# Two heads of an attention tile: their TensorE products issued head after head, or by turns

## The chip, the core and the metric

The kernel runs on one core of one Trainium2 chip. A core has five engines, each with an instruction queue of its own, that wait for each other through semaphores: TensorE (PE in the profile, its weight loads in a row of their own, PEld), VectorE (DVE), ScalarE (ACT), GpSimd (POOL) and SyncE (SP, which here only issues DMA transfers). The metric is the device time of one execution in microseconds (us); lower is better.

## The reference, cut to what matters

The reference is one decoder layer over 256 tokens of width 2048, in float32: a SwiGLU feed-forward half-step, a mixer, and a second feed-forward half-step, each followed by a layer normalisation. The mixer projects the tokens into queries, keys, values and the input of a convolution branch. Attention and convolution are computed from these and joined by one output projection.

Attention has 16 query heads of 64 features and 2 key and value heads. Tokens stand in two blocks of 128. A query of block b sees keys of block b-1 and of its own block, no more than 127 tokens back:

```
scores = einsum('bnqhgd,bnkhd->bnhgqk', qb, kb) * ATTN_SCALE
scores = where(valid, scores, finfo(float32).min)
probs  = softmax(concatenate([scores, sink], -1), -1)[..., :-1]
out    = einsum('bnhgqk,bnkhd->bnqhgd', probs, vb)
```

The convolution branch takes a gated product, runs a causal depthwise convolution of 31 taps over it, normalises and applies SiLU.

## The kernel before, in words

**Weights.** Every weight arrives by DMA as float32, in pieces of 128 x 1024. Each piece is split into a rounded part `hi` (ScalarE, line 126) and a remainder `lo` (line 128, on VectorE, or on GpSimd for some pieces of the mixer). TensorE multiplies with both (lines 384 to 386: hi by hi, the two cross products, no lo by lo). The class `Steps` hands the pieces out: `take()` gives the next piece, `release()` gives its buffer back, `step()` ends a step of the program, splits up to two pieces ahead, and calls work that was put off with `st.at(delay, work)`. Each engine is given its instructions in the order in which this Python text issues them; no planner moves them. `st.tensor` and `st.vector` only count, on the host, how much work VectorE has outstanding, to decide at which step convolution taps are issued.

**The mixer.** First a product over tokens gives keys, values and the queries of the first two tiles. Then 14 items follow in the order `ccqqccqqccqqcc`: a "c" is one 128-channel tile of the convolution branch (two products of 48 matmuls, then a sigmoid on ScalarE, line 661, and a gated product on VectorE, line 662), a "q" is the query tile of two heads (one product of 48 matmuls, then a copy with bias on ScalarE, line 762). After every two "c" tiles VectorE gets two chains of 31 taps (line 653). In between, the pieces of attention come due.

**Attention.** There are 8 tiles. Tile `i` holds two heads: head 0 in partitions 0 to 63 of `qT` and `kT`, head 1 in partitions 64 to 127. `attend(i)` puts the scores of a tile into one PSUM tile `sc` of 128 x 2 x 512, head `h` in `sc[:, h]`, a bank of its own. In each bank columns 0 to 127 belong to query block 0 and columns 128 to 383 to query block 1. Three matmuls make a head's scores: the mask, as identity times mask in bf16 over 384 columns (line 677), which also clears the bank, then the product of block 0 (line 678, 128 columns), then that of block 1 (line 679, 256 columns), both in float32 and adding to the mask. A float32 matmul is executed as two loads of weights and two passes, so lines 678 and 679 each show 32 instructions for 16 calls.

From there the steps of `ATT` follow, some 1, 1, 2, 2, 4, 6 and 7 steps after `attend`: the maximum (VectorE, line 691), the exponentials (ScalarE, line 701), the sums and reciprocal (VectorE, lines 708 and 709), the division (ScalarE, line 715), the transposes `turn` (TensorE, line 721) with their copy `pT` (ScalarE, line 724), the product with the values (TensorE, lines 733 to 735) and the copy of the result (lines 740 and 741).

`values()` multiplies the transposed shares by `v`. The weights are the 64 columns of `v` of the head (`v[..][:, r]`), so head 0 writes partitions 0 to 63 of the result and head 1 partitions 64 to 127. Per head there are three float32 matmuls of 128 columns, each again two loads and two passes.

After the 14 items the first half of the output projection starts (`tokens_by`, product lines 384 to 386 on `mh` and `ml`), while VectorE still works on the last two chains of taps.

Of the kernel before, what the change touches and what calls it, by code (L numbers as in the profile page):

```python
# [18 lines left out]
P = 128  # L19
# [8 lines left out]
HD = 64  # L28
# [545 lines left out]
def mixer(tc, nc, env):  # L574
# [6 lines left out]
    with tc.tile_pool(name="mix", bufs=1) as pool:  # L581
# [11 lines left out]
        v = [kvq[:, b, P : 2 * P] for b in range(2)]  # L593
# [3 lines left out]
        def turn_first():  # L597
            tq = psA.tile([P, 2, 512], F32, tag="gu", name="tq")
            for b in range(2):
                for n, col in enumerate((0, 2, 3)):  # L600
                    nc.tensor.transpose(
                        tq[:, n // 2, (n % 2) * S + b * P : (n % 2) * S + (b + 1) * P],
                        kvq[:, b, col * P : (col + 1) * P], ident,
                    )
            nc.scalar.copy(kT, tq[:, 0, :S])
            nc.scalar.copy(qTs[0], tq[:, 0, S:])
            nc.scalar.copy(qTs[1], tq[:, 1, :S])
            attend(0)
            st.at(3, lambda: attend(1))
# [62 lines left out]
        def attend(i):  # L672
            qT = qTs.pop(i)
            sc = psA.tile([P, 2, 512], F32, tag="gu", name="sc")
            for h in range(2):
                r = slice(h * HD, (h + 1) * HD)
                nc.tensor.matmul(sc[:, h, : 3 * P], ident_b, mask, start=True, stop=False)
                nc.tensor.matmul(sc[:, h, :P], qT[r, :P], kT[r, :P], start=False, stop=False)
                nc.tensor.matmul(sc[:, h, P : 3 * P], qT[r, P:], kT[r, :], start=False, stop=True)
            mx = small.tile([P, 2, 2], F32, tag="mx", name="mx")  # L680
            nm = small.tile([P, 2, 2], F32, tag="nm", name="nm")
            se = small.tile([P, 2, 2], F32, tag="se", name="se")
            sm = small.tile([P, 2, 2], F32, tag="sm", name="sm")
            pr = pool.tile([P, 2, 3 * P], F32, tag="pr", name="pr", bufs=2)
            pT = pool.tile([P, 2, 3 * P], F32, tag="pT", name="pT", bufs=2)
            tps = []
            st.tensor(1.6)

            def most():
                for b in range(2):  # L690
                    nc.vector.tensor_reduce(out=mx[:, b], in_=sc[:, :, spans[b]], axis=AX.X, op=ALU.max)
                nc.vector.scalar_tensor_tensor(
                    out=nm, in0=mx, scalar=-SCALE, in1=nsink[:, i], op0=ALU.mult, op1=ALU.min
                )
                nc.vector.tensor_tensor(out=se, in0=psink[:, i], in1=nm, op=ALU.add)
                st.vector(1.5)

            def exps():
                for h in range(2):
                    for b in range(2):  # L700
                        nc.scalar.activation(
                            pr[:, h, spans[b]], sc[:, h, spans[b]], AF.Exp, bias=nm[:, b, h : h + 1], scale=SCALE,
                            accum_out=sm[:, b, h : h + 1],
                        )
                nc.scalar.activation(se, se, AF.Exp)

            def shares():
                nc.vector.tensor_tensor(out=sm, in0=sm, in1=se, op=ALU.add)
                nc.vector.reciprocal(sm, sm)
                st.vector(0.3)  # L710

            def divide():
                for h in range(2):
                    for b in range(2):
                        nc.scalar.mul(pr[:, h, spans[b]], pr[:, h, spans[b]], sm[:, b, h : h + 1])

            def turn():
                tp = psA.tile([P, 2, 512], F32, tag="gu", name="tp")
                for h in range(2):
                    for n in range(3):  # L720
                        nc.tensor.transpose(
                            tp[:, h, n * P : (n + 1) * P], pr[:, h, n * P : (n + 1) * P], ident
                        )
                nc.scalar.copy(pT, tp[:, :, : 3 * P])
                st.tensor(0.7)
                tps.append(tp)

            def values():
                o = tps[0][:, :, 3 * P :]
                st.tensor(0.9)  # L730
                for h in range(2):
                    r = slice(h * HD, (h + 1) * HD)
                    nc.tensor.matmul(o[r, 0], v[0][:, r], pT[:, h, :P], start=True, stop=True)
                    nc.tensor.matmul(o[r, 1], v[0][:, r], pT[:, h, P : 2 * P], start=True, stop=False)
                    nc.tensor.matmul(o[r, 1], v[1][:, r], pT[:, h, 2 * P :], start=False, stop=True)

            def keep():
                o = tps[0][:, :, 3 * P :]
                m = [x_[:, i].rearrange("p (b n) -> p b n", b=2) for x_ in (mh, ml)]
                nc.scalar.copy(m[0], o)  # L740
                nc.vector.tensor_tensor(out=m[1], in0=o, in1=m[0].bitcast(F32), op=ALU.subtract)
                st.vector(0.35)

            for n, (work, after) in zip(
                ATT, ((most, False), (exps, True), (shares, False), (divide, True), (turn, False), (values, False), (keep, False))
            ):
                st.at(n, work, after)
# [3 lines left out]
        for kind in ORDER:  # L751
            ps = psB.tile([P, 512], F32, tag="acc", name=f"in_{kind}")
            features(ps[:, :S])
            if kind == "c":
                st.step()
                features(ps[:, S:])
                glu(nconv, ps)
                nconv += 1
                st.step()
            else:  # L760
                qTs[nq] = pool.tile([P, S], F32, tag="qT", name="qT", bufs=3)
                nc.scalar.activation(qTs[nq], ps[:, :S], AF.Identity, bias=bias[:, nq : nq + 1])
                st.at(2, lambda i=nq: attend(i))
                nq += 1
                st.step()
# [143 lines left out]
```

## Time and profile before

| | |
|---|---|
| time, median of 3 runs | 1785.87 us (1784.53 to 1787.3) |
| the profiled execution | 1784.28 us, of which 1782.5 us from the first to the last instruction |
| TensorE matmuls | busy 1747.7 us, 98% of the span |
| TensorE weight loads | busy 1512.8 us, 85% |
| VectorE | busy 1054.7 us, 59% |
| ScalarE | busy 830.5 us, 47% |
| GpSimd | busy 141.8 us, 8% |
| mean granted TensorE clock | 0.995 |
| first and last start of a score matmul | 772.8 and 906.7 us |
| first and last start of a values matmul | 796.1 and 927.9 us |

Matmuls are pipelined: a matmul's own duration is longer than its distance to the next one, so distances between starts say what a matmul costs, and a busy share of 98% doesn't say that the engine is at its peak. "Idle before" and a name behind an arrow give the time in which an engine had nothing running, and what ended it. Forms such as 64*128 give the rows and columns of the weights that a matmul uses.

### The profile page before, as it was taken

Reading aid. Unit: us, or ns where it says so; the run is one execution under the profiler, and the core shown is the slowest. Engines: PE = TensorE matmul, PEld = TensorE weight load, DVE = VectorE, ACT = ScalarE, POOL = GpSimd, SP = SyncE. Lnnn points to the kernel's source line nnn. Section 1 sums busy time; section 2 is a strip of 40 time slices with the busy share of each in tenths; the row PEclk is TensorE's granted clock in tenths of the full one; section 3 lists DMA queues with packets and bytes.
Section 4 is the critical chain, followed back from the end, with each engine's and each line's share of the span. In section 5 each row is a group of like instructions: output and inputs, shape, how many; then the busy total and the mean of one; then the engine's idle time right before and its main releaser. Section 6 shows DMA issues by size and latency. Waiting matters only on the chain.

```text
span 1782.5 us, 23512 instructions
## 1 busy us (share of the span) xinstructions
PE 1747.7 (98%) x9550; PEld 1512.8 (85%) x9550; DVE 1054.7 (59%) x1386; ACT 830.5 (47%) x1145; POOL 141.8 (8%) x82
## 2 busy tenths in 40 slices
PE   8999999999999999999998999999999999999997
PEld 6888888888888888789997778888888888888885
DVE  5555555445555555658889676755555445555546
ACT  5544444334444433575653474544443434444441
POOL 0000000000000000205654420000000000000000
PEclk9999999999999999999999999999999999999998
DMA  8655555555555555445544445655555555555651
GB/s 313 237 189 190 190 189 208 190 193 183 189 190 189 190 208 192 145 164 176 182 145 166 165 165 179 226 190 191 190 207 189 191 187 189 190 189 189 239 209 48
DMA packets 52092, 336.48 MB, mean 189 GB/s; under 512 B 6288, under 2 KB 6416, under 8 KB 13072
## 3 DMA queue, kind: packets, MB, share of 16 engines
q1 hardware_dynamic: 51984, 334.98, 53.7%
q8 instruction: 75, 1.23, 0.3%
q14 instruction: 33, 0.27, 0.0%
HBM read 332.86 MB, written 2.10 MB: 188 GB/s over the span
## 4 chain that ended last, share of the span: by engine, by line
PE 92%; DVE 4%; DMA 2%; ACT 1%; issue 1%; SPq 0%; DVEq 0%; ACTq 0%
PE gu L492 32%; PE gu L501 17%; PE acc L384 10%; PE acc L385 10%; PE acc L386 10%; PE in_c L384 2%; PE in_c L385 2%; PE in_c L386 2%; DMA rb<-in_rows 2%; PE grp L386 1%; PE grp L385 1%; PE grp L384 1%; DVE lo L128 1%; DVE z L325 1%; PE in_q L384 1%
## 5 line engine op out<-in xcount | busy, mean ns | idle before, releaser
L128 DVE TENSOR_TENSOR lo<-raw,hi 128x1024 fp32r<-128x1024 f32 (+1 forms) x569 | 695.3, 1238 | 520.1 <-issue 285.3
L126 ACT CAST hi<-raw 128x1024 fp32r<-128x1024 f32 (+1 forms) x614 | 633.4, 1047 | 335.2 <-PE acc L386 319.6
L492 PE MATMUL gu<-xcat,hi 128*128 128x512 f32 x2688 | 626.0, 390 | 0.5 <-ACT hi L126 0.5
L492 PEld LDWEIGHTS gu<-xcat,hi 128*128 128x128 f32 x2688 | 499.3, 188 | 101.2 <-ACT hi L126 1.0
L501 PEld LDWEIGHTS gu<-xcat,lo 128*128 128x128 f32 x2688 | 333.6, 192 | 6.5
L501 PE MATMUL gu<-xcat,lo 128*128 128x256 f32 x2688 | 335.6, 283 | 0.0
L384 PE MATMUL acc<-hi,hh 128*128 128x512 f32 x704 | 274.6, 390 | 0.0
L385 PE MATMUL acc<-lo,hh 128*128 128x512 f32 x704 | 274.4, 390 | 0.0
L386 PE MATMUL acc<-hi,hl 128*128 128x512 f32 x704 | 274.3, 390 | 0.0
L514 ACT COPY corr<-gu 128x512 f32<-128x512 f32 x84 | 49.3, 586 | 438.5 <-PE gu L501 438.5
L128 POOL TENSOR_TENSOR lo<-raw,hi 128x1024 fp32r<-128x1024 f32 x45 | 112.0, 2498 | 808.3 <-ACT hi L126 808.2
L386 PEld LDWEIGHTS acc<-hi,hl 128*128 128x128 f32 x704 | 132.5, 188 | 27.7
L384 PEld LDWEIGHTS acc<-hi,hh 128*128 128x128 f32 x704 | 132.5, 188 | 27.5
L385 PEld LDWEIGHTS acc<-lo,hh 128*128 128x128 f32 x704 | 132.5, 188 | 26.8
L515 DVE TENSOR_TENSOR both<-gu,corr 128x512 f32<-128x512 f32 x84 | 58.0, 691 | 84.2 <-ACT corr L514 84.2
L653 DVE SCALAR_TENSOR_TENSOR conv<-hc,cw_sb,conv 128x256 f32<-128x256 f32 x232 | 93.4, 479 | 3.2 <-ACT conv L649 3.2
L384 PE MATMUL in_c<-xcat,hi 128*128 128x256 f32 x256 | 73.9, 289 | 0.0
L386 PE MATMUL in_c<-xcat,lo 128*128 128x256 f32 x256 | 72.4, 283 | 0.0
L385 PE MATMUL in_c<-xcat,hi 128*128 128x256 f32 x256 | 72.4, 283 | 0.0
L265 DVE SCALAR_TENSOR_TENSOR xt<-acc,xt 128x512 f32<-128x512 f32 x48 | 32.9, 689 | 57.0 <-PE acc L386 57.0
L384 PE MATMUL acc<-hi,mh 128*128 128x512 f32 x128 | 51.2, 400 | 6.9 <-DVE xt L265 4.6
L384 PEld LDWEIGHTS in_c<-xcat,hi 128*128 128x128 f32 x256 | 49.0, 191 | 2.4 <-issue 2.3
(125 smaller groups left out, 1122.2 us busy)
## 6 DMA issues: line engine op xcount, KB each, us to landing
raw<-in_wu SPq DMA_DIRECT2D x168, 1024.0 KB, 4.8
raw<-in_wd SPq DMA_DIRECT2D x88, 1024.0 KB, 4.8
raw<-in_win SPq DMA_DIRECT2D x26, 1024.0 KB, 4.9
raw<-in_wout SPq DMA_DIRECT2D x16, 1024.0 KB, 4.8
raw<-in_wt SPq DMA_DIRECT2D x4, 1024.0 KB, 4.8
raw<-in_wt SPq DMA_DIRECT2D x6, 512.0 KB, 6.8
xt<-in_x SPq DMA_DIRECT2D x2, 1024.0 KB, 7.5
rg<-in_rows SPq DMA_DIRECT2D x8, 256.0 KB, 5.1
```

Source lines behind the costliest of these rows:

```text
L126: nc.scalar.copy(hi, raw)
L128: eng.tensor_tensor(out=lo, in0=raw, in1=hi.bitcast(F32), op=ALU.subtract)
L265: nc.vector.scalar_tensor_tensor(out=y, in0=ps, scalar=factor, in1=y, op0=ALU.mult, op1=ALU.add)
L325: nc.vector.tensor_scalar(out=z, in0=xt[:, b, c * 512 : (c + 1) * 512], scalar1=mv[:, 0:1], scalar2=r, op0=ALU.subtract, op1=ALU.mult,)
L384: nc.tensor.matmul(ps, s_hi, m_hi, start=start, stop=False)
L385: nc.tensor.matmul(ps, s_hi, m_lo, start=False, stop=False)
L386: nc.tensor.matmul(ps, s_lo, m_hi, start=False, stop=stop)
L492: nc.tensor.matmul(gu[:, m, :], parts[n4][0][:, q * P : (q + 1) * P], xc[:, k].rearrange("p a n -> p (a n)"), start=k == 0, stop=False,)
L501: nc.tensor.matmul(gu[:, m, S:], parts[n4][1][:, q * P : (q + 1) * P], xc[:, k, 0, :], start=False, stop=k == KT - 1,)
L514: nc.scalar.copy(corr, gu[:, :, S:])
L515: nc.vector.tensor_tensor(out=both, in0=gu[:, :, :S], in1=corr, op=ALU.add)
L653: nc.vector.scalar_tensor_tensor(out=acc if k < CK - 1 else cv[:, i], in0=hc[:, k : k + S], scalar=cw_sb[:, i, k : k + 1], in1=acc, op0=AL ...
```

## The change

In `attend`, the masks of both heads are issued first, then line 678 for head 0 and head 1, then line 679 for head 0 and head 1. In `values`, the three matmuls of the two heads are issued by turns: the first of head 0 and of head 1, the second of both, the third of both. The matmuls themselves, their operands, targets and accumulation flags stay the same, and so do their number, everything on the other engines, and the DMA transfers.

```diff
         def attend(i):
             qT = qTs.pop(i)
             sc = psA.tile([P, 2, 512], F32, tag="gu", name="sc")
+
+            rows = [slice(h * HD, (h + 1) * HD) for h in range(2)]
             for h in range(2):
-                r = slice(h * HD, (h + 1) * HD)
                 nc.tensor.matmul(sc[:, h, : 3 * P], ident_b, mask, start=True, stop=False)
+            for h, r in enumerate(rows):
                 nc.tensor.matmul(sc[:, h, :P], qT[r, :P], kT[r, :P], start=False, stop=False)
+            for h, r in enumerate(rows):
                 nc.tensor.matmul(sc[:, h, P : 3 * P], qT[r, P:], kT[r, :], start=False, stop=True)
...
             def values():
                 o = tps[0][:, :, 3 * P :]
                 st.tensor(0.9)
-                for h in range(2):
-                    r = slice(h * HD, (h + 1) * HD)
-                    nc.tensor.matmul(o[r, 0], v[0][:, r], pT[:, h, :P], start=True, stop=True)
-                    nc.tensor.matmul(o[r, 1], v[0][:, r], pT[:, h, P : 2 * P], start=True, stop=False)
-                    nc.tensor.matmul(o[r, 1], v[1][:, r], pT[:, h, 2 * P :], start=False, stop=True)
+                rows = [slice(h * HD, (h + 1) * HD) for h in range(2)]
+                for n, (ob, vb, start, stop) in enumerate(((0, 0, True, True), (1, 0, True, False), (1, 1, False, True))):
+                    for h, r in enumerate(rows):
+                        nc.tensor.matmul(o[r, ob], v[vb][:, r], pT[:, h, n * P : (n + 1) * P], start=start, stop=stop)
```

## The prediction

> **What bounds the kernel now.** I read the page first, its busy times and its chain of the work that ended last.
>
> ```profile
> span 1782.5 us, 23512 instructions
> PE 1747.7 (98%) x9550; PEld 1512.8 (85%) x9550; DVE 1054.7 (59%) x1386; ACT 830.5 (47%) x1145; POOL 141.8 (8%) x82
> PE 92%; DVE 4%; DMA 2%; ACT 1%; issue 1%; SPq 0%; DVEq 0%; ACTq 0%
> ```
>
> TensorE sets the time: 92% of the chain is matmul. So a microsecond taken from TensorE counts, unless TensorE then waits for something that was just in time. Next I read what TensorE waits for from the mixer to the next feed-forward (757 to 1060 us).
>
> ```profile
> PE acc L384 <- DVE xt L265: 4.6, 1, 4.6
> PE sc L678 <- ACT qT L606: 0.6, 1, 0.6
> ```
>
> In the stretch that the change touches, 772 to 932 us, only the second wait lies, at the first tile. The first, at 946 us, comes later and matters below: there TensorE waits for VectorE.
>
> **The work touched.** The groups by line and shape of the same stretch give the counts (busy us, mean ns):
>
> ```profile
> L679 PE MATMUL sc<-kT,qT 64*128 64x256 f32 x32 | 9.5, 377 | 0.0
> L678 PE MATMUL sc<-kT,qT 64*128 64x128 f32 x32 | 7.8, 322 | 0.6 <-ACT qT L606 0.6
> L733 PE MATMUL tp<-pT,kvq 128*64 128x128 f32 x32 | 5.7, 298 | 0.0
> L677 PE MATMUL sc<-mask,ident_b 128*128 128x384 bf16 x16 | 5.4, 336 | 0.0
> ```
>
> Means of pipelined matmuls overlap, so I cost by distances between starts, in the timeline of TensorE. One tile's scores (start, us, operation; the last two rows are single passes of its first head, seen in narrow windows):
>
> ```profile
> 810.49 0.28 PE L385 MATMUL in_q<-xcat,hi 128*128 128x256 f32 x1
> 810.61 0.28 PE L386 MATMUL in_q<-xcat,lo 128*128 128x256 f32 x1
> 810.73 0.34 PE L677 MATMUL sc<-mask,ident_b 128*128 128x384 bf16 x1
> 810.99 0.49 PE L678 MATMUL sc<-kT,qT 64*128 64x128 f32 x2
> 811.32 0.59 PE L679 MATMUL sc<-kT,qT 64*128 64x256 f32 x2
> 811.85 0.34 PE L677 MATMUL sc<-mask,ident_b 128*128 128x384 bf16 x1
> ...
> 812.96 0.39 PE L384 MATMUL in_q<-xcat,hi 128*128 128x256 f32 x1
> 811.21 0.27 PE L678 MATMUL sc<-kT,qT 64*128 64x128 f32 x1
> 811.54 0.38 PE L679 MATMUL sc<-kT,qT 64*128 64x256 f32 x1
> ```
>
> The reader sees a mask of 0.26 (810.73 to 810.99), one head's products of 0.86 (to 811.85), and the same again for the other head, 1.11 (to 812.96): 2.23 in all. A head's products start 0.00, 0.22, 0.33 and 0.55 into their piece and the next mask follows 0.31 after the last. A pass of 256 columns takes 0.22 there (0.55 - 0.33), so 0.09 of the 0.31 is the array emptying before it goes from 64 rows back to 128; and the first pass costs 0.11 more than the second (0.22 against 0.11), its load, which nothing covers. No two products of different heads lie side by side here: the full-height mask of head 1 stands between them.
>
> **Scores, worked out.** After the change the second mask follows the first in the same mode, then both heads' products run in the 64-row mode without a full-height matmul between. The second mask's price has no row of its own: 256 columns go every 0.12 (810.49 to 810.61), so 384 columns are an estimated 0.17. It is then 0.17 + 0.26 + 0.86 + lag, where the lag is by how much head 1's products trail head 0's. They use the other 64 rows and a bank of their own. The sum 1.29 + lag against 2.23 saves 0.94 - lag for each tile. The first tile is different:
>
> ```profile
> 772.83 0.33 PE L677 MATMUL sc<-mask,ident_b 128*128 128x384 bf16 x1
> 773.73 0.48 PE L678 MATMUL sc<-kT,qT 64*128 64x128 f32 x2 [0.57 <-ACT qT L606]
> 775.69 0.39 PE L384 MATMUL in_c<-xcat,hi 128*128 128x256 f32 x1
> ```
>
> Its second mask hides in the wait for `qT`, which shrinks from 0.57 to about 0.40: 0.90 + 0.86 + lag against 2.86 saves 1.10 - lag.
>
> **The lag** for two row groups is in no row of this trace, because of that mask. The nearest rows are those of the values, where the heads use two column groups:
>
> ```profile
> 796.13 0.43 PE L733 MATMUL tp<-pT,kvq 128*64 128x128 f32 x2
> 796.41 0.32 PE L733 MATMUL tp<-pT,kvq 128*64 128x128 f32 x1
> 796.51 0.27 PE L734 MATMUL tp<-pT,kvq 128*64 128x128 f32 x1
> 796.57 0.27 PE L733 MATMUL tp<-pT,kvq 128*64 128x128 f32 x1
> 796.62 0.27 PE L735 MATMUL tp<-pT,kvq 128*64 128x128 f32 x1
> 796.90 0.38 PE L735 MATMUL tp<-pT,kvq 128*64 128x128 f32 x2
> 797.21 0.39 PE L384 MATMUL in_c<-xcat,hi 128*128 128x256 f32 x1
> ```
>
> Each head issues 733, 733, 734, 734, 735, 735 one head after the other, yet a third 733 starts at 796.41, ahead of a 734 and the first 735: head 1 already overtakes head 0 and runs beside it. Each keeps its own pace (0.16 from first to second pass in both: 796.41 to 796.57, and 0.43 - 0.27 for head 0), so column groups don't slow each other. Loads neither, at one place at least (weight loads of both heads in flight):
>
> ```profile
> 796.40 0.14 PEld L734 LDWEIGHTS tp<-pT,kvq 128*64 128x64 f32 x1
> 796.41 0.13 PEld L733 LDWEIGHTS tp<-pT,kvq 128*64 128x64 f32 x1
> ```
>
> They give the lag's lower end, 0.00: the engine can start two groups' loads within 0.01. The upper end is one pass, 0.11 (796.51 to 796.62), if head 1 must wait until head 0's second load, issued ahead of it, has gone. I take 0.05, between them.
>
> **Values, worked out.** Head 1 now trails by 0.28 (796.13 to 796.41), since head 0's loads and passes stand ahead of it in the queue. By turns only the first two pairs do. With the same lag each tile saves 0.28 - 0.05 = 0.23.
>
> **The sum for TensorE.** Scores 7 x 0.89 + 1.05 = 7.28, values 8 x 0.23 = 1.84, together 9.12. With a lag of 0.00 it is 6.58 + 1.10 + 2.24 = 9.92, with 0.11 it is 5.81 + 0.99 + 1.36 = 8.16.
>
> In the Trainium skill, "TensorE: Matmul & The Clock Gate", section "Part 3: Packing small matmuls", the span of packed matmuls is one matmul plus about 4 ns for each further tile; by that the sum would be near the 9.92. The rows above agree for loads (0.01) and leave it open for rows.
>
> **What it triggers.** VectorE and ScalarE must follow. The splits have room: the last weight piece of the 14 items was ready at 919.35 and is first used at about 928.1.
>
> ```profile
> 916.95 2.40 POOL L128 TENSOR_TENSOR lo<-raw,hi 128x1024 fp32r<-128x1024 f32 x1 [4.42 <-ACT hi L126]
> 928.11 0.39 PE L384 MATMUL in_c<-xcat,hi 128*128 128x256 f32 x1
> ```
>
> The tightest wait of TensorE on attention's own chain is the last tile's transposes, behind the division:
>
> ```profile
> 916.74 1.51 ACT L715 ACTIVATE pr<-pr,sm 128x128 f32<-128x128 f32 x4
> 920.48 0.87 PE L721 MATMUL tp<-ident,pr 128*128 128x128 f32 x6
> ```
>
> 2.23 us of room (918.25 to 920.48) against 2 x 0.89 + 0.23 = 2.01 gained since the last point where VectorE waited for TensorE. It just fits. These points, where VectorE idles for the gated product of a "c" tile, are:
>
> ```profile
> 845.79 0.49 DVE L662 SCALAR_TENSOR_TENSOR hc<-in_c,bias,sg 128x256 f32<-128x256 f32 x1 [2.14 <-ACT sg L661]
> 888.79 0.48 DVE L662 SCALAR_TENSOR_TENSOR hc<-in_c,bias,sg 128x256 f32<-128x256 f32 x1 [1.51 <-ACT sg L661]
> 931.80 0.48 DVE L662 SCALAR_TENSOR_TENSOR hc<-in_c,bias,sg 128x256 f32<-128x256 f32 x1 [1.97 <-ACT sg L661]
> ...
> 863.70 0.16 DVE L708 TENSOR_TENSOR sm<-sm,se 128x4 f32<-128x4 f32 x1 [1.02 <-ACT se L705]
> ```
>
> Between two of them lie two tiles, so TensorE gains 2 x (0.89 + 0.23) = 2.24, and VectorE can only come forward by its idle time. To 845.79 that is 2.14 and more earlier; to 888.79 it is 1.51 and some of the 1.02 at 863.70, whose exponentials stand on ScalarE behind work that TensorE released; to 931.80 it is 1.97. From 931.80 VectorE's chains of taps lead to the wait at 946 us, so what VectorE doesn't follow is lost there. I charge 2.24 - 1.97 = 0.27. If none of the 1.02 follows, 2.24 - 1.51 = 0.73 more is lost.
>
> Forecast gain: 9.12 - 0.27 = 8.85. Ends: 9.92 - 0.47 (pairs of tiles gain 2.44) = 9.45; at lag 0.11 pairs gain 2.00, 8.16 - 0.03 - 0.49 = 7.64. The profiled execution took 1784.28, which gives 1775.4; it lies 1.59 under the median of the runs, and against that median, 1785.87, the gain gives **1777.0**, with 1776.4 to 1778.2 by the two ends. The three runs lie 1.3 under to 1.4 over their median, so the likeliest case alone has 1775.1 to 1779.6.
>
> **Rivals.** First, *starts stay in program order* and a head's pass can't start before the other head's pass ahead of it. Scores then start at 0.00, 0.22 (head 0), 0.22, 0.33 (head 1), 0.33, 0.55, 0.55, 0.77 and end 0.31 later: 1.08 instead of 0.86, which saves 0.72 each, first tile 0.88, so 5.92. Values: 0, 0.16, 0.16, 0.27, 0.27, 0.38, 0.38, 0.49, 0.49, 0.60, 0.60, 0.71, then 0.20 as at the end of the rows shown (the second of the last two 735 starts 0.11 after 796.90, the next matmul at 797.21): 0.91 against 1.08, 8 x 0.17 = 1.36. Gain 7.28 with nothing held back (pairs gain 1.78, under 1.97): 1778.6. Against it: the 733 at 796.41 starts ahead of 734 and 735 issued before it.
>
> The Trainium skill's "TensorE: Matmul & The Clock Gate", same section, says that matmuls start and end strictly in program order. By that rule this rival holds; this trace disagrees for column groups, and no run here shows row groups yet.
>
> Second, *the change doesn't do what it says for the values*: the engine brings the heads together itself, whatever the order, and its head start of 0.28 has another cause, such as a start-up. Then scores alone gain 7.28, again nothing held back: 1778.6. For it: the overtaking is there now. Against: head 1's first load goes within 0.01 of head 0's fourth, as one would see if it stood behind head 0's instructions.
>
> Third, *row groups take turns*, pipelined like one head's passes: starts 0, 0.22, 0.33, 0.44, 0.55, 0.77, 0.99, 1.21, end 1.52. A tile takes 0.17 + 0.26 + 1.52 = 1.95, saves 0.28; the first 2.86 - 2.42 = 0.44; 2.40 in all, and values 1.84: 1781.6. For it: no row shows two row groups together.
>
> Fourth, the **slower side**: *every change of row group empties the array*, as going from mask to products does. The place is the products of lines 678 and 679, which now change group three times instead of being split once by a mask. A piece of two short passes is 0.22 + 0.11 + 0.09 = 0.42, one of two long ones 0.11 + 0.22 + 0.22 + 0.09 = 0.64. A tile takes 0.17 + 0.26 + 2 x (0.42 + 0.64) = 2.55, 0.32 more than 2.23; the first 0.90 + 2.12 - 2.86 = 0.16 more: 7 x 0.32 + 0.16 = 2.40 more in all, values unchanged since they overlap as it is: 1788.3. It decides once each of the three changes costs more than 0.09, a third of the 0.28 that plain turns still save; priced as here it costs 0.20 (0.09 of emptying, 0.11 of uncovered load). Against: the column groups change without a gap.
>
> **How the numbers follow.** Side by side 0.67, program order 0.10, values unchanged 0.11, turns 0.08, turns with emptying 0.04. The time is the first one's, 1777.0. The range runs from 1774.7, just under the likeliest case's own end, to 1781.7, which takes in the third; left out are the fourth, half of the third and the tails. A measurement of this kernel can tell about 0.2% (3.6 us) from no change. Under 1782.3 lie the first three cases and most of the turns, faster 0.92; the rest of the turns and the fourth's 1788.3 are within, 0.06; 0.02 for emptying that costs more than the 0.20 I gave it.
>
> **What would show it.** Right: from the mask's start to the next projection matmul 1.34 us instead of 2.23, with 678 and 679 of both heads interleaved and a head's own pace kept; values from first 733 to next matmul 0.85 instead of 1.08; the wait for `qT` about 0.40; VectorE's idle time at the last gated product near zero. Wrong: passes of 678 at 0.22 apart throughout, gaps of 0.1 and more between heads, a wait of the last transposes on the division of over 0.3, or a wait at 946 us that grows by more than 0.5.

## The result, and the profile after

The changed kernel takes **1775.74 us** (median of 6 runs, 1773.88 to 1777.11) against 1786.12 of the kernel before (6 runs, 1784.53 to 1787.3). The ratio is 0.9944 with a 95% interval of 0.9933 to 0.9954: 10.4 us less, within 8.2 to 12.0. The forecast was 1777.0, a gain of 8.85.

From the page of the changed kernel, its span, busy times and the chain that ended last:

```profile
span 1772.1 us, 23512 instructions
PE 1737.9 (98%) x9550; PEld 1505.8 (85%) x9550; DVE 1053.8 (59%) x1386; ACT 830.5 (47%) x1145; POOL 143.4 (8%) x82
PE 95%; DVE 3%; ACT 1%; DMA 1%; issue 0%; SPq 0%; DVEq 0%; ACTq 0%
```

The same 9550 matmuls and as many loads, 9.8 us less of TensorE's busy time. What TensorE waits for from the mixer to the next feed-forward (us in total, times, longest), after:

```profile
PE acc L384 <- DVE xt L265: 4.6, 1, 4.6
...
PE acc L384 <- ACT mh L806: 2.3, 1, 2.3
...
PE sc L680 <- ACT qT L606: 0.4, 1, 0.4
```

No wait is new, and the one for `qT` went from 0.6 to 0.4. The scores of the tile that the prediction showed, in TensorE's timeline after the change (line 678 is now the mask, 680 and 682 are the products; x4 stands for both heads):

```profile
806.58 0.28 PE L386 MATMUL in_q<-xcat,lo 128*128 128x256 f32 x1
806.70 0.50 PE L678 MATMUL sc<-mask,ident_b 128*128 128x384 bf16 x2
807.13 0.49 PE L680 MATMUL sc<-kT,qT 64*128 64x128 f32 x4
807.45 0.60 PE L682 MATMUL sc<-kT,qT 64*128 64x256 f32 x4
807.98 0.39 PE L384 MATMUL in_q<-xcat,hi 128*128 128x256 f32 x1
```

Mask to next projection matmul: 1.28 us (806.70 to 807.98) instead of 2.23. The products of both heads take 0.85 (807.13 to 807.98), what one head's took alone: the heads run side by side and the second one costs nothing that this view can show. In the unrounded starts head 1's passes follow head 0's by 0.006 us in every tile. The first tile, and one tile's values (line 737 holds all 12 passes):

```profile
772.29 0.49 PE L680 MATMUL sc<-kT,qT 64*128 64x128 f32 x4 [0.41 <-ACT qT L606]
773.15 0.38 PE L384 MATMUL in_c<-xcat,hi 128*128 128x256 f32 x1
...
792.43 0.28 PE L386 MATMUL in_c<-xcat,lo 128*128 128x256 f32 x1
792.64 0.88 PE L737 MATMUL tp<-pT,kvq 128*64 128x128 f32 x12
793.44 0.39 PE L384 MATMUL in_c<-xcat,hi 128*128 128x256 f32 x1
```

The values take 0.80 from their first pass to the next matmul instead of 1.08.

**Where the time went, by stretch.** From each profile I took four points in TensorE's timeline: the last transpose ahead of the first mask, the first matmul behind the last values, the last transpose of the next normalisation, the end. The table gives what lies between them (us).

| kernel | to the first mask | attention | behind it, to the normalisation | rest | span |
|---|---|---|---|---|---|
| before | 772.72 | 155.39 | 118.76 | 735.63 | 1782.5 |
| before, second profile | 772.81 | 155.39 | 119.00 | 734.79 | 1782.0 |
| changed | 771.28 | 145.51 | 120.11 | 735.20 | 1772.1 |
| changed, second profile | 772.07 | 145.51 | 120.11 | 734.81 | 1772.5 |

Attention gained **9.88 us**, the same in both pairs of profiles. Of this, 1.1 to 1.4 us are lost again in the stretch behind it. The first and last columns lie outside the change; they differ by up to 0.8 between two profiles of one kernel. So the profiles show 8.5 to 8.8 us less, and the median's 10.4 is higher. Its interval reaches down to 8.2. A second comparison, below, gave 0.9937, with an interval that reaches down to 9.1 us.

The granted clock of the runs suggests where the difference comes from. The kernel before ran 33 times beside the experiments; one of these runs was slow, at 3632.47 us, and is left out here. Of the other 32, 21 have a mean granted clock of 0.993 or 0.994 and 11 one of 0.995 to 0.997. Its two profiled executions, at 0.995 and 0.996, have a clock like the smaller group's. At 0.994 the kernel before takes 1785.84 us (mean of 19 runs) and the changed kernel 1775.96 (mean of 3); at 0.995 they take 1784.17 (4 runs) and 1774.19 (5). At equal clock the gain is thus 9.9 to 10.0 us, about what the attention gained. The groups are small and the clock is given in steps of 0.001, so this is an estimate. By it the loss behind the attention belongs to the executions that were profiled, and not to the change in every run.

### The profile page after: what moved, and what is told of

Read it like the earlier page. It is cut to its first block, busy times and chain, and to the rows that moved or that the text cites. A ratio compares the mean times of both kernels' runs of the same rounds, so it can differ in the third digit from the quotient of the medians.

```text
span 1772.1 us, 23512 instructions
## 1 busy us (share of the span) xinstructions
PE 1737.9 (98%) x9550; PEld 1505.8 (85%) x9550; DVE 1053.8 (59%) x1386; ACT 830.5 (47%) x1145; POOL 143.4 (8%) x82
## 4 chain that ended last, share of the span: by engine, by line
PE 95%; DVE 3%; ACT 1%; DMA 1%; issue 0%; SPq 0%; DVEq 0%; ACTq 0%
PE gu L492 34%; PE gu L501 18%; PE acc L384 10%; PE acc L385 10%; PE acc L386 10%; PE in_c L384 2%; PE in_c L385 2%; PE in_c L386 2%; PE grp L386 1%; PE grp L384 1%; PE grp L385 1%; PE in_q L384 1%; DVE z L325 1%; PE in_q L385 1%; PE in_q L386 1%; DVE conv L653 0%
## 5 line engine op out<-in xcount | busy, mean ns | idle before, releaser
L386 PE MATMUL acc<-hi,ml 128*128 128x512 f32 x128 | 51.1, 399 | 0.0
```

The lines of the kernel that those rows point to most:

```text
L386: nc.tensor.matmul(ps, s_lo, m_hi, start=False, stop=stop)
```

## The experiments

### Scores alone, values alone

The first kernel has the change in `attend` and the old `values`, the second the other way round.

> Only the scores are changed (masks first, products by turns); the values stay head after head. Theory: the heads' products run side by side with a lag of 0.006 us, so TensorE saves 0.95 us in each of 7 tiles and 1.11 in the first, 7.75 in all between 772 and 932 us, and VectorE follows: 7.8 us under the kernel before, about 1778.3. From the matmul ahead of the first mask to the matmul behind the last product 1.41 us instead of 2.36; values still 1.28. Rival: the gain beyond the forecast hangs on the values, because only both together move VectorE's short operations out of GpSimd's way; then the scores alone give 6.5 us or less.

> Only the values are changed (by turns); the scores stay as before. Theory: 0.27 us for each of 8 tiles, 2.15 in all, about 1784.0, hard to tell from no change by the time; in the trace 1.02 us instead of 1.28 from the matmul before the first product to the one behind the last. Rival that the change does nothing for the values, since the engine brings the heads together itself: 1.28 stays, 1786.1.

Measured: scores alone 1776.93 against 1785.04, ratio 0.9957 (0.9944 to 0.997), and 147.64 us for the attention's stretch, a gain of **7.75**. Values alone 1782.71, ratio 0.9988 (0.998 to 0.9997), stretch 153.26, a gain of **2.13**. Both parts are what their matmuls save, and they add up to the 9.88 of the full change. The rival that one part needs the other to move VectorE falls, and so does the rival that the change does nothing for the values.

### Does it take turns? Heads one after the other behind both masks

```diff
-            for h, r in enumerate(rows):
-                nc.tensor.matmul(sc[:, h, :P], qT[r, :P], kT[r, :P], start=False, stop=False)
             for h, r in enumerate(rows):
+                nc.tensor.matmul(sc[:, h, :P], qT[r, :P], kT[r, :P], start=False, stop=False)
                 nc.tensor.matmul(sc[:, h, P : 3 * P], qT[r, P:], kT[r, :], start=False, stop=True)
...
+                for some in ((0, 1), (2,)):
+                    for h, r in enumerate(rows):
+                        for n in some:
```

> Both masks first, but then the products head after head (lines 678 and 679 of head 0, then of head 1); the values with two products of head 0, two of head 1, then one of each. Theory that the engine looks past about five instructions that haven't started: eight instructions of head 0 stand ahead of head 1 in both places, of which the first two start at once, so the lag is 0.11 or less for scores and 0.06 or less for values. Scores gain 7.0 to 7.8 us, values 1.7 to 2.2, the time is within 1.2 us of the full change, about 1776.5. Rival, that the turns themselves matter: head 1 starts when head 0's last load has gone, a lag of 0.33 for scores (gain 5.2 us) and 0.17 or more for values (gain 0.9), about 1780. Second rival, strict program order of starts: a lag of 0.55 or more in the scores, gain 3.5 us or less, about 1782.

Measured: 1775.05 us, ratio 0.9945 (0.9931 to 0.9959), stretch 145.62, 0.11 from the full change. The scores of the same tile in this kernel (680 and 681 are the products):

```profile
807.11 0.50 PE L678 MATMUL sc<-mask,ident_b 128*128 128x384 bf16 x2
807.54 0.50 PE L680 MATMUL sc<-kT,qT 64*128 64x128 f32 x4
807.87 0.61 PE L681 MATMUL sc<-kT,qT 64*128 64x256 f32 x4
808.40 0.39 PE L384 MATMUL in_q<-xcat,hi 128*128 128x256 f32 x1
```

0.86 for both heads: with eight instructions of head 0 ahead of head 1, the lag is 0.013 us (0.014 in the values), against 0.006 with four. **For the scores the turns weren't needed; moving the second mask was.** Both rivals fall.

### Where the reach ends: three products a head

```diff
+            for h, r in enumerate(rows):
+                nc.tensor.matmul(sc[:, h, :P], qT[r, :P], kT[r, :P], start=False, stop=False)
+                for c in range(2):
+                    nc.tensor.matmul(
+                        sc[:, h, (c + 1) * P : (c + 2) * P], qT[r, P:], kT[r, c * P : (c + 1) * P], start=False, stop=c == 1
+                    )
```

> The changed kernel, but the scores' products head after head behind both masks, and line 679's product cut into two of 128 columns, so that 12 instructions of head 0 stand ahead of head 1. Theory that the engine reaches past six instructions that haven't started, and not past seven: head 1 can start only when head 0's third pass has, a lag of 0.33 us instead of 0.01; the scores take 1.73 us instead of 1.41 and the stretch of the attention 148.0 to 148.2 us. Rival, that for row groups every instruction ahead costs 1.6 ns and nothing else: a lag of 0.02, 145.6.

One run, 1778.9 us; stretch 148.10. The same tile:

```profile
808.74 0.50 PE L678 MATMUL sc<-mask,ident_b 128*128 128x384 bf16 x2
809.16 0.49 PE L680 MATMUL sc<-kT,qT 64*128 64x128 f32 x2
809.49 0.27 PE L682 MATMUL sc<-kT,qT 64*128 64x128 f32 x1
809.50 0.37 PE L680 MATMUL sc<-kT,qT 64*128 64x128 f32 x1
809.60 0.27 PE L682 MATMUL sc<-kT,qT 64*128 64x128 f32 x1
809.71 0.27 PE L680 MATMUL sc<-kT,qT 64*128 64x128 f32 x1
...
810.36 0.39 PE L384 MATMUL in_q<-xcat,hi 128*128 128x256 f32 x1
```

Head 1's first pass (the 680 at 809.50) starts together with head 0's third (809.49), a lag of 0.33 as expected, and TensorE's array has one head alone until then. By reach I mean how many of one head's loads and passes TensorE passes over to start the other head's. The loss of the old values, a lag of 0.28 with 12 instructions ahead, appears in the row groups as well once 12 stand ahead. The limit by itself isn't visible in a trace; a reach past six instructions that haven't started, and not past seven, fits all four cases (8 and 12 instructions ahead, for scores and for values).

### VectorE and GpSimd

> The kernel before, in which the remainders that GpSimd computes are replaced by a copy on ScalarE; the subtraction of those pieces is left out, so the outputs differ from the reference's. Theory: VectorE's operations on two SBUF operands stand still while GpSimd works on its own; without those the longest of the small operations on the maxima falls from 1.25 us (0.79 the next) to at most 0.3, the longest remainder on VectorE from 2.92 to at most 2.5 (GpSimd keeps the residual's operations), and VectorE is busy 137 to 140 us instead of 144.3 in the attention's stretch. Rival, that the long ones waited for an input: they stay.

```diff
-            eng = nc.gpsimd if n in self.pooled else nc.vector
-            eng.tensor_tensor(out=lo, in0=raw, in1=hi.bitcast(F32), op=ALU.subtract)
-            if eng is nc.vector:
+            if n in self.pooled:
+                nc.scalar.copy(lo, raw)
+            else:
+                nc.vector.tensor_tensor(out=lo, in0=raw, in1=hi.bitcast(F32), op=ALU.subtract)
                 self.vector(1.14)
```

The small operations on the maxima in this kernel, and the remainders on VectorE in its stretch from 772 to 932 us (ns min/median/max):

```profile
L693 DVE SCALAR_TENSOR_TENSOR nm<-mx,nsink x8: 161/162/164, 775.8 to 911.5; 128x4 f32<-128x4 f32 x8
...
L130 DVE TENSOR_TENSOR lo<-raw,hi x22: 1205/1224/1489, 773.5 to 926.4; 128x1024 fp32r<-128x1024 f32 x22
```

One run, 1782.2 us. The longest small operation is 0.16 us instead of 1.25, the longest remainder 1.49 instead of 2.92. VectorE's durations in the attention's stretch sum to 138.1 us (144.3 before, 140.9 changed). TensorE's stretch stays at 155.39. The theory holds: those operations stood still for GpSimd's work, and the rival, a late input, falls.

### The clock behind the waits

> The kernel before once more, for a second profile. Theory that its first profile met the higher clock behind the two waits by chance: from the first of them (at 946 us) to the transposes of the next normalisation it takes about 1 to 2 us more this time, as in every other profile of this study (100.1 us there, 101.4 to 103.0 elsewhere). Rival, that the earlier arrival costs the changed kernel its clock: 100.1 again. Either way the stretch from the first score to behind the last values is 155.4.

Measured: one run, 1783.76 us; 155.39 us for the attention, and 100.3 from the first wait to the transposes (100.1 in its first profile; the table's column adds the 18.7 ahead of the wait, so 119.00 and 118.76). The profiles speak against chance: in that column the kernel before has at most 119.0 twice, and the kernels with an earlier arrival and these waits as they are have 120.1 to 121.7. The runs don't rule it out, since their granted clock differs within one kernel, as told with the result. To see what the clock costs, the two waits were filled in the changed kernel:

```diff
+            if n in warm:
+                dummy = psA.tile([P, 2, 512], F32, tag="gu", name="warm")
+                for _ in range(warm[n]):
+                    nc.tensor.matmul(dummy[:, 0, : 3 * P], ident_b, mask, start=True, stop=True)
...
-        tokens_by((mh, ml), 0, NT, 1.0, None, None)
+        tokens_by((mh, ml), 0, NT, 1.0, None, None, {4: 18})
...
-            (mh, ml), NT, NT, 1.0, stats, lambda b: env["norm_to_features"](b, stats, env["par2"], 2, x2)
+            (mh, ml), NT, NT, 1.0, stats, lambda b: env["norm_to_features"](b, stats, env["par2"], 2, x2), {0: 8}
```

> The changed kernel, and in two waits behind the attention 18 and 8 matmuls of identity times mask whose result nobody reads: ahead of the second column group of the output projection's first half (the wait of 4.6 us at 935) and ahead of its second half (2.3 us at 977). Theory: the matmuls behind these waits ran at 0.43 us apart instead of 0.23 because TensorE's clock had been lowered while it waited, and that this cost more after the change than before; kept busy, the clock stays up, the slow matmuls (8 and 7 there) nearly vanish, and the kernel gains 2 to 3 us on the changed one, about 1773. Rival: they are slow since the load and the operands come late, whatever TensorE did before; then the time stays, or is up to 1 us longer.

> The changed kernel with the two waits filled by 18 and 8 unread matmuls, again, now beside the changed kernel itself. Theory: 2.0 to 3.3 us faster than it, with the stretch behind the values at 117.4 to 117.6 in the profile and a smaller spread between runs. Rival, that the difference seen between two calls was one between chips: under 1 us.

> The changed kernel once more, beside the one with filled waits on the same chip, and for a second profile. Theory: the attention's stretch is 145.5 us again, and the time about 10 us under the kernel before. If TensorE's lowered clock behind the two waits is a matter of chance, the stretch from behind the last values to the next normalisation's last transposes lies somewhere between 118.8 and 121.7, as in the profiles so far; if the earlier arrival itself sets it, it is 120.1 again.

The first of these kernels took 1772.43 against 1785.73 before, ratio 0.9929 (0.9915 to 0.9943). Beside each other on one chip: filled 1772.46 (1771.62 to 1772.97), changed 1774.26 (1772.92 to 1775.54), before 1784.54; the ratios to before are 0.9927 (0.9913 to 0.994) and 0.9937 (0.9924 to 0.9949). The stretch behind the attention is 117.45 and 117.43 filled, 120.11 unfilled. The views by stretch of time behind the two waits (us, busy times and counts of the engines, then the granted clock, DMA share, GB/s), kernel before:

```profile
946.00:952.00 6.00, 5.22 (x17) 4.26 (x18) 6.00 (x14) 0.81 (x1) 0.00 (x0) 0.72 0.50 180
988.00:992.00 4.00, 3.45 (x14) 2.56 (x15) 1.92 (x4) 3.97 (x8) 0.69 (x1) 1.00 0.74 264
```

Changed:

```profile
935.00:941.00 6.00, 5.53 (x17) 4.45 (x18) 6.00 (x14) 0.86 (x1) 0.00 (x0) 0.72 0.54 195
977.00:981.00 4.00, 3.76 (x9) 2.71 (x10) 1.88 (x3) 3.97 (x8) 0.73 (x1) 0.57 0.75 264
```

Changed, waits filled:

```profile
935.00:941.00 6.00, 4.42 (x19) 3.67 (x20) 6.00 (x14) 1.05 (x1) 0.20 (x1) 1.00 0.56 186
977.00:981.00 4.00, 3.73 (x16) 2.76 (x16) 1.70 (x4) 3.97 (x8) 1.20 (x1) 1.00 0.67 254
```

In the four microseconds behind the second wait the kernel before had the full clock and 14 matmuls, the changed one 0.57 and 9, the filled one full clock and 16 (its wait ended 0.2 us ahead of that stretch, the others' 0.2 to 0.3 us into it). So the clock falls with a wait and unread matmuls keep it up; that is worth 2.7 us of the stretch in the profiles and 1.8 in the medians, whose intervals overlap, a little under the 2.0 to 3.3 expected. The filled kernel has the lowest median of this study. The second profile of the changed kernel gave 120.11 once more.

Why the same wait of 2.32 us leaves the clock up in the kernel before and not in the changed one can be read from narrower views. Behind the attention each stretch of half clock lasts 3.41 us or twice that, and within one profile such stretches begin a whole number of steps of 3.41 us apart (changed kernel: at 936.17 and 977.13, twelve steps). These are the steps around the second wait, the changed kernel's two and then those of the kernel before, counted on from its half clock at 946.24 (same columns as above):

```profile
973.72:977.12 3.40, 1.20 (x6) 0.65 (x4) 2.65 (x4) 3.37 (x8) 0.00 (x0) 1.00 0.00 0
977.13:980.53 3.40, 3.29 (x7) 2.33 (x8) 1.75 (x3) 3.37 (x8) 0.26 (x1) 0.50 0.87 308
...
983.79:987.19 3.40, 2.17 (x14) 1.58 (x12) 1.77 (x3) 3.37 (x9) 0.00 (x0) 1.00 0.00 0
987.20:990.60 3.40, 2.05 (x8) 1.40 (x9) 2.31 (x5) 3.34 (x9) 0.00 (x0) 1.00 0.60 198
```

In the changed kernel 2.2 us of the wait lie in one step, TensorE is busy for only 1.20 of it, and the next step has half the clock. In the kernel before the wait lies across the border of two steps, TensorE is busy for 2.17 and 2.05 of them, and the clock stays up. The other profiles of kernels with unfilled waits fit: in the seven in which the clock fell behind this wait, 2.1 to 2.3 us of it lay in the step ahead of the fall; in the two in which it stayed, those of the kernel before, no step held more than 1.2 and 1.5 us of it. The number of steps at half clock orders the stretches behind the attention:

| profiles | steps at half clock, first wait | second wait | stretch behind the attention, us |
|---|---|---|---|
| changed, waits filled (two) | 0 | 0 | 117.43, 117.45 |
| before (two) | 1 | 0 | 118.76, 119.00 |
| changed (two) | 1 | 1 | 120.11, 120.11 |
| heads after masks, values alone, three products, scores alone | 2 | 1 | 120.56, 121.18, 121.58, 121.69 |

The kernel without GpSimd's remainders, with other work and a shorter first wait (4.07 us), has 2 and 1 and takes 118.81. So an earlier arrival doesn't cost the clock by itself: with the values alone TensorE arrives 2.1 us earlier than before and loses more than the full change, which brings it 9.9 earlier. What counts in these profiles is how each wait lies on the steps. Why the first wait costs one step in some profiles and two in others is open.

The Trainium skill, "TensorE: Matmul & The Clock Gate", section "Part 1: The HAM clock gate", says that the clock is halved after an idle window of about 3.4 us, at a phase that the kernel doesn't set. The steps of 3.41 us and the matmuls 0.43 apart instead of 0.23 agree with that. A whole idle window wasn't needed here: 2.1 to 2.3 us of idle time in one step were enough.

## Why the prediction was right, and where it wasn't

**The terms of TensorE.** The second mask was put at 0.17, and its start is 0.173 behind the first's. The first tile saved 1.11 (the forecast was 1.10 less the lag). **The mis-sized term is the lag**, put at 0.05 between the ends 0.00 and 0.11, and measured at 0.006: 7 x 0.949 + 1.111 + 8 x 0.269 = 9.9 instead of 9.12. The rows of two weight loads 0.01 apart were the right ones to go by. The upper end rested on head 1 having to wait for head 0's second load; the kernel with eight instructions ahead shows that it needn't.

In the Trainium skill's "TensorE: Matmul & The Clock Gate", section "Part 3: Packing small matmuls", the span rule with 4 ns a tile was nearer than my 0.05, and the rows now agree with it for row groups, 6 ns here. The section's other rule, strict program order of starts, is at odds with these runs in both kinds of groups: the 680 of head 1 at 809.50 starts ahead of the 682 at 809.60 that stands before it.

**The term of VectorE failed.** I charged 0.27 because VectorE "can only come forward by its idle time". At the first of the three gated products that the prediction names it had no idle time left, but it kept up: at the last one 0.96 us were left, where the prediction's sign was "near zero" (DVE, changed kernel).

```profile
839.87 0.47 DVE L662 SCALAR_TENSOR_TENSOR hc<-in_c,bias,sg 128x256 f32<-128x256 f32 x1
879.91 0.48 DVE L662 SCALAR_TENSOR_TENSOR hc<-in_c,bias,sg 128x256 f32<-128x256 f32 x1 [1.11 <-ACT sg L661]
920.49 0.48 DVE L662 SCALAR_TENSOR_TENSOR hc<-in_c,bias,sg 128x256 f32<-128x256 f32 x1 [0.96 <-ACT sg L661]
```

It came forward in its busy time too. VectorE and GpSimd at one tile's maxima, and two remainders of VectorE, before:

```profile
904.77 1.25 DVE L692 SCALAR_TENSOR_TENSOR nm<-mx,nsink 128x4 f32<-128x4 f32 x1
906.05 1.19 DVE L695 TENSOR_TENSOR se<-psink,nm 128x4 f32<-128x4 f32 x1
...
903.62 2.37 POOL L128 TENSOR_TENSOR lo<-raw,hi 128x1024 fp32r<-128x1024 f32 x1 [4.49 <-ACT hi L126]
905.96 1.26 POOL L357 TENSOR_TENSOR xt<-xt,rg 128x512 f32<-128x512 f32 x1
...
884.37 2.92 DVE L128 TENSOR_TENSOR lo<-raw,hi 128x1024 fp32r<-128x1024 f32 x1
...
927.19 1.86 DVE L128 TENSOR_TENSOR lo<-raw,hi 128x1024 fp32r<-128x1024 f32 x1
```

After:

```profile
895.91 0.28 DVE L695 SCALAR_TENSOR_TENSOR nm<-mx,nsink 128x4 f32<-128x4 f32 x1
896.22 1.21 DVE L698 TENSOR_TENSOR se<-psink,nm 128x4 f32<-128x4 f32 x1
...
893.80 2.37 POOL L128 TENSOR_TENSOR lo<-raw,hi 128x1024 fp32r<-128x1024 f32 x1 [3.52 <-ACT hi L126]
896.13 1.28 POOL L357 TENSOR_TENSOR xt<-xt,rg 128x512 f32<-128x512 f32 x1
...
876.98 1.83 DVE L128 TENSOR_TENSOR lo<-raw,hi 128x1024 fp32r<-128x1024 f32 x1
...
917.39 1.35 DVE L128 TENSOR_TENSOR lo<-raw,hi 128x1024 fp32r<-128x1024 f32 x1
```

An operation on four columns that takes 0.16 alone ends when GpSimd's does, within 0.03 us each time. Before, it met a remainder 1.2 us ahead of its end; after, 0.26. This one and two remainders (2.92 to 1.83 and 1.86 to 1.35 us) gave VectorE 2.6 us between the gated products at 845.79 and 931.80 of the kernel before, where I had counted idle time alone.

The Trainium skill's "SBUF — State Buffer", section "SBUF: two separate sides", has this as a lock: a VectorE operation with two SBUF inputs and one of GpSimd that reads SBUF exclude each other for a whole instruction. The rows and the kernel without GpSimd's remainders agree with it; I should have read 1.25 us on four columns that way.

**What I left out.** The wait at 946 us stayed at 4.6 and only moved, where the forecast let it grow by 0.27. But I didn't ask what TensorE's clock does behind it, and in the profiled executions that took 1.1 to 1.4 back. The forecast of 8.85 lies 1.03 under the 9.88 that the attention gained: 0.76 by the lag and 0.27 by VectorE. That it stands close to the profiles' 8.5 to 8.8 is luck, since those two errors and the loss left out nearly cancel there.

**The other cover held.** The last tile's transposes still didn't wait for the division (changed kernel, ScalarE and TensorE):

```profile
906.95 1.51 ACT L718 ACTIVATE pr<-pr,sm 128x128 f32<-128x128 f32 x4
...
909.43 0.88 PE L724 MATMUL tp<-ident,pr 128*128 128x128 f32 x6
```

The room went from 2.23 to 0.97 us, not to the 0.2 that the sum left, since VectorE and ScalarE came forward.

**The rivals.** Starts in program order, row groups by turns, and emptying at each change of row group are all refuted by one head's 0.85 for both heads. The one on the values is refuted by 0.80 instead of 1.08, and by the kernel with values alone.

## What to carry to other kernels

Small float32 products of different heads overlap on TensorE if they use different rows or columns of the array; a full-height matmul between them, here a mask, keeps them apart and costs more than their order, so put such matmuls together and the small ones behind them. Up to two float32 products of one head may stand ahead of the other's; with three, taking turns pays, 0.27 us each time. Where TensorE waits a few microseconds anyway, look at the clock of the matmuls behind the wait, and count VectorE's stretched operations as room beside its idle time.

## What the runs showed of the hardware that I had not expected

The engine reaches over eight instructions of one group for 0.013 us, about 1.6 ns each, but with 12 ahead the lag jumps to 0.28 or 0.33. A wait of 2.32 us cost the clock in one kernel and not in another whose work there is the same, each time in both of their profiles, by how it lay on steps of 3.41 us.
